# Modulation as plain float32 products in four column tiles

## The chip, the cores and the metric

The kernel runs on one core of one Trainium2 chip. The metric is the device time of one execution in microseconds; the median of three runs of the kernel before is 2310.57 us (2305.61 to 2311.26). TensorE (PE) multiplies, VectorE (DVE), ScalarE (ACT) and GpSimd (POOL) work elementwise, and SyncE (SP) issues most of the DMAs, in order.

## The reference

One inference step of a two-layer trunk on 128 context tokens and 512 latent tokens of width 1024, all in float32. In each layer the input is normalised and modulated, `h = rms_norm(x, g) * (1 + scale) + shift`; `h` goes through one wide projection into four mixers (two softmax attentions with several heads, a differential attention, a state-space scan), gates, and merges; the result is projected and added back, `x = x + gate * out`.

What matters here is where `shift`, `scale` and `gate` come from:

```
sh, sc, ga = split(silu(c) @ w_mod[l] + b_mod[l], 3)     # once for the context c_ctx, once for the latent c
```

`w_mod[l]` is 1024 x 3072 in float32, so each layer multiplies two vectors by a 12.6 MB matrix.

## The kernel before, in words

Activations are held feature-major, 128 features by 640 tokens. Products are made to float32 precision out of float32r operands: each operand is split into a high part (`fhi`, rounded by ACT, line 130) and a low part (`flo`, the difference, line 131, on the engine that is passed in), and three products hi·hi, hi·lo, lo·hi are added (lines 148 to 152). `w_chunk` (line 133) does that for a 256 KB block of weights: a DMA on SP into a raw tile (`fraw`), ACT makes `fhi`, POOL or DVE makes `flo`. The tag `f` has 3 raw buffers and 4 of each part, and is used by gates, merges, branch outputs and several projections (`fm_halves`, line 699: 48 matmuls of 320 columns for two blocks, in two halves, 0.146 us apart).

`modulation(l, part)` (line 214) makes one third of the modulation of a layer. For each half `ch` of 512 output columns it takes 8 blocks of 128 x 512 weights. Each block is split, and the four columns of `s4` (high and low parts of the two conditioning vectors) are the stationary operand: one matmul of 512 columns against `hi` (line 229) and one against `lo` (line 230), into 4 rows of a PSUM bank. The rows are copied or added to `row` (lines 232, 234), four 4 x 128 transposes (line 239) turn them to columns, and three to five small DVE operations finish `mod` (lines 241 to 248).

It is called in two ways.

- With `pool`, ahead of layer 0: parts 0 and 1 (shift and scale), 32 blocks with tag `m` (8 raw buffers, 4 of each part), all eight blocks of a half in one accumulation. The low parts go to DVE for two blocks in three and to POOL for the third. This stage is ordered by the compiler's planner on every engine. `h` (lines 1317 to 1319) waits for both parts of its half, and the first projection (`tm_proj`, lines 174 to 176) for `h`.
- Without `pool`, beside the gates and merges (tag `f`): part 2 of layer 0 and parts 0 and 1 of layer 1 in layer 0, part 2 of layer 1 in layer 1: 64 blocks, two to an accumulation, so 32 bursts of four matmuls. `mix(project(3, 0), chain(*mod), 8)` puts a burst after every eight steps of the merge and branch-output products; these in turn are dealt out between the pieces of the attentions by `fill`. From the end of the first stage on, PE runs in the order in which the program is written; the other engines and the DMA queues are still ordered by the planner.

Of the kernel before, what the change touches and what calls it, by code (L numbers as in the profile page):

```python
# [12 lines left out]
F32 = mybir.dt.float32  # L13
F32R = mybir.dt.float32r
AF = mybir.ActivationFunctionType
ALU = mybir.AluOpType
AX = mybir.AxisListType

P = 128
DEPTH = 2  # L20
D = 1024
KD = 8
# [3 lines left out]
TC = (0, 128, 384, 512, 256)  # L26
EPS = 1e-6
MLA_SCALE = 96 ** -0.5
WB = {"w": (2, 2), "f": (3, 4), "m": (8, 4)}
PTB = 3  # L30
PB = 2
TB = 3
# [23 lines left out]
def hybrid_kernel(ctx: ExitStack, tc: tile.TileContext, A, O, dbg=None):  # L56
    nc = tc.nc
    V, S, G, T = nc.vector, nc.scalar, nc.gpsimd, nc.tensor

    cp = ctx.enter_context(tc.tile_pool(name="cp", bufs=1))  # L60
    wp = ctx.enter_context(tc.tile_pool(name="wp", bufs=2))
# [5 lines left out]
    def nm(s):  # L67
        uid[0] += 1
        return f"{s}_{uid[0]}"

    def taker(pool):
        def take(tag, shape, bufs=1, dt=F32):
            return pool.tile(shape, dt, tag=tag, name=nm(tag), bufs=bufs)
        return take

    ct = taker(cp)

    def f(ap):
        return ap.bitcast(F32)

    def load(dst, src):
        nc.sync.dma_start(dst, src)
        return dst
# [6 lines left out]
    ident = ct("ident", [P, P])  # L90
# [18 lines left out]
    def psum_mm():  # L109
        return ps.tile([P, 512], F32, tag="mm", name=nm("mm"), bufs=2)  # L110
# [17 lines left out]
    def split_to(hi, lo, src, eng=V):  # L128

        S.activation(hi, src, AF.Copy)  # L130
        eng.tensor_tensor(lo, src, f(hi), ALU.subtract)  # L131

    def w_chunk(src, shape, eng=V, t="w", pool=wp):

        raw = load(pool.tile(shape, F32, tag=t + "raw", name=nm(t + "raw"), bufs=WB[t][0]), src)
        hi, lo = (pool.tile(shape, F32R, tag=t + n, name=nm(t + n), bufs=WB[t][1]) for n in ("hi", "lo"))
        split_to(hi, lo, raw, eng)
        return hi, lo
# [66 lines left out]
    sT = ct("sT", [P, KD, 2])  # L205
    S.activation(sT, cc, AF.Tanh, scale=0.5)
    V.scalar_tensor_tensor(sT, sT, 1.0, cc, op0=ALU.add, op1=ALU.mult)
    V.tensor_scalar(sT, sT, 0.5, None, op0=ALU.mult)
    s4 = ct("s4", [P, KD, 2, 2], 1, F32R)
    split_to(s4[:, :, :, 0], s4[:, :, :, 1], sT)  # L210

    mods = {}

    def modulation(l, part, group=2, pool=None):


        mod = mods[l, part] = ct(f"mod{part}", [P, KD, 2], 2)
        gcol = load(ct("gcol", [P, KD], 2), A["ng"][l]) if part == 1 else None
        bm = load(ct("bm", [P, KD], 2), A["bmod"][l, part])
        pt = ct("mpt", [P, KD, 4], 2)  # L220
        for ch in range(2):
            row = ct("mrow", [4, 512])
            for k0 in range(0, KD, group):
                acc = psum_mm()
                for k in range(k0, k0 + group):
                    src = A["wmod"][l, 2 * part + ch, k]
                    whi, wlo = w_chunk(src, [P, 512], V if k % 3 else G, "m", pool) if pool else w_chunk(src, [P, 512], G, "f")
                    lhs = s4[:, k].rearrange("p a b -> p (a b)")
                    T.matmul(acc[0:4, :], lhsT=lhs, rhs=whi, start=k == k0, stop=False)
                    T.matmul(acc[0:4, :], lhsT=lhs, rhs=wlo, start=False, stop=k == k0 + group - 1)  # L230
                if k0 == 0:
                    S.activation(row, acc[0:4, :], AF.Copy)
                else:
                    V.tensor_tensor(row, row, acc[0:4, :], ALU.add)
                if not pool:
                    yield
            tr = psum_mm()
            for q in range(4):
                T.transpose(tr[:, 4 * q:4 * q + 4], row[:, q * P:(q + 1) * P], ident[0:4, 0:4])
            c = slice(4 * ch, 4 * ch + 4)  # L240
            V.tensor_copy(pt[:, c], tr[:, 0:16].rearrange("p (m s) -> p m s", s=4))
            pv, m = pt[:, c].rearrange("p m (s t) -> p m s t", t=2), mod[:, c]
            V.tensor_tensor(m, pv[:, :, :, 0], pv[:, :, :, 1], ALU.add)
            V.tensor_tensor(m, m, bm[:, c].unsqueeze(2).to_broadcast([P, 4, 2]), ALU.add)
            if part == 1:
                V.scalar_tensor_tensor(m, m, 1.0, gcol[:, c].unsqueeze(2).to_broadcast([P, 4, 2]), op0=ALU.add, op1=ALU.mult)
            if part == 2:
                V.tensor_scalar(m, m, 0.25, None, op0=ALU.mult)
            if pool:
                yield  # L250
# [1038 lines left out]
    acc = xat("acc", [P, NT])  # L1289
# [12 lines left out]
    for l in range(DEPTH):  # L1302
# [3 lines left out]
        if l == 0:  # L1306
            mstack, mp = open_pool("m0")
            first = [modulation(0, i, KD, mp) for i in range(2)]
# [4 lines left out]
        for k in range(KD):  # L1313
            sh, sc = mods[l, 0], mods[l, 1]
            t = xat("ht", [P, NT], 2)
# [57 lines left out]
        for i in range(8):  # L1373
            nc.sync.dma_start(ucm[64:80, :, i], usb[16 * i:16 * i + 16])
            src = outs[i // 2][64 * (i % 2):64 * (i % 2) + 64].rearrange("p (g n) -> p g n", n=16)
# [20 lines left out]
        for ft in range(4):  # L1396
# [3 lines left out]
            pv = py[:, :, 0:320].rearrange("p h (i c) -> p h i c", c=80)  # L1400
# [29 lines left out]
        kstack, kp = open_pool(f"k{l}")  # L1430
        at = lambda tag, *a, takers=(taker(bp), taker(kp)): takers[tag in ("k", "q", "v")](tag, *a)
        mod = [modulation(l, 2)] + ([] if last else [modulation(l + 1, i) for i in range(2)])

        def project(n, i):
# [5 lines left out]
        b = []  # L1440
# [22 lines left out]
        for d_ in range(KD):  # L1463
            bo = fm_tile(A["wbo"][l, 1, d_], *b, 4, G)
            t = load(xat("ht", [P, NT], 2), ttd[l][1][d_])
            pv = load(xat("sq", [P, NT], 2), mgd[l][2][d_])
# [5 lines left out]
        acc = xat("acc", [P, NT])  # L1472
# [22 lines left out]
def cols(x):  # L1495

    t, f_ = x.shape
    return x.reshape(t // 8, 8, f_)[:, ::-1].reshape(t // 8, 2, 4, f_).transpose(1, 2, 0, 3).reshape(2, t // 2, f_)
# [17 lines left out]
def host_inputs(x):  # L1516
    x = {k: np.asarray(v) for k, v in x.items()}
    c = np.ascontiguousarray
    o = {}
# [20 lines left out]
    w = x["w_in"]  # L1540
    a = np.cumsum([0, 256, 128, 32, 512, 512, 512, 512, 128, 128, 512, 2048, 4096])
# [44 lines left out]
    b = np.stack([x["ssm_b_re"], x["ssm_b_im"]], 1)  # L1586
# [18 lines left out]
    def tmj(t):  # L1605
        return c(cols(t).reshape(4, P, -1).transpose(1, 0, 2))

    o["tk"] = c(np.stack([np.concatenate([tmj(cF), tmj(cM)], -1), np.concatenate([tmj(sF), tmj(sM)], -1)], 1))
    o["blk"] = c(np.repeat(np.eye(4, dtype=np.float32), 32, 0))
    return o  # L1610

# [39 lines left out]
```

## Time and profile before

| | |
|---|---|
| median of three runs | 2310.57 us |
| profiled execution | 2309.3 us, span 2307.5 us |
| granted TensorE clock, mean | 0.961 of full speed |
| PE busy | 2109.0 us (91%) |
| DVE busy | 1375.3 us (60%) |
| ACT busy | 1031.0 us (45%) |
| POOL busy | 905.1 us (39%) |
| DMA | 400.60 MB, mean 174 GB/s |

The busy share is a mean over stages. In the view of stretches a row gives its bounds in us, its length, the busy us of each engine with the count of instructions, the granted clock (1.00 is 2.4 GHz), the share of the DMA engines that was busy, and the rate. Matmuls overlap in the pipeline, so the cost of one in a stream is read from the difference of two starts, not from its duration.

### The profile page before, as it was taken

The numbers are of one execution on the slowest core, as the hardware profiler recorded it, in microseconds if no ns is written. First come the engines' busy times: TensorE is split into PE (matmuls) and PEld (weight loads), VectorE is DVE, ScalarE is ACT, GpSimd is POOL, SyncE is SP. The second block draws the span as 40 slices with busy tenths as digits, with TensorE's granted clock in tenths as the row PEclk, the third lists the DMA queues.
The fourth block names the chain that finished last, engine by engine and source line by source line (L and its number), as shares of the span: only waits on it lengthen the run. The fifth ranks groups of instructions, "written<-read, shape, count | busy, mean of one in ns | idle before, by whom it ended". The sixth has DMA issues, their size and how long they took to land. (4 is left out here: it accounts for less than half of the span.)

```text
span 2307.5 us, 38266 instructions
## 1 busy us (share of the span) xinstructions
PE 2109.0 (91%) x14197; PEld 2010.3 (87%) x14197; DVE 1375.3 (60%) x2515; ACT 1031.0 (45%) x2069; POOL 905.1 (39%) x637
## 2 busy tenths in 40 slices
PE   5876889969999999998799999997999999999997
PEld 2876789969998889998788999897899899999997
DVE  7998672755455455665777685349345455565542
ACT  5332343314556665553233444341346656554332
POOL 4477431312335552345553364232132523234522
PEclk9988999989999999999899999998999999999998
DMA  6455576533745666666473386763384455566643
GB/s 219 118 189 200 183 240 189 175 90 120 214 140 152 179 193 181 182 196 198 155 252 129 117 249 217 248 180 93 102 249 131 148 149 156 174 188 184 201 148 116
DMA packets 238635, 400.60 MB, mean 174 GB/s; under 512 B 36400, under 2 KB 110128, under 8 KB 238448
## 3 DMA queue, kind: packets, MB, share of 16 engines
q1 hardware_dynamic: 224208, 372.13, 53.5%
q10 hardware_dynamic: 14240, 26.02, 3.1%
q8 instruction: 111, 1.82, 0.4%
q14 instruction: 76, 0.62, 0.1%
HBM read 279.67 MB, written 117.87 MB: 172 GB/s over the span
## 5 line engine op out<-in xcount | busy, mean ns | idle before, releaser
L131 POOL TENSOR_TENSOR flo<-fraw,fhi 128x512 fp32r<-128x512 f32 x368 | 528.4, 1443 | 897.4 <-ACT fhi L130 850.4
L148 PE MATMUL mm<-hhi,fhi 128*128 128x320 f32 x2048 | 667.2, 326 | 25.2 <-DVE gt L764 7.5
L152 PE MATMUL mm<-hhi,flo 128*128 128x320 f32 x2048 | 640.8, 313 | 7.0 <-POOL flo L131 7.0
L150 PE MATMUL mm<-hlo,fhi 128*128 128x320 f32 x2048 | 639.8, 312 | 0.0
L148 PEld LDWEIGHTS mm<-hhi,fhi 128*128 128x128 f32 x2048 | 393.7, 192 | 38.3 <-ACT rx L942 8.0
L152 PEld LDWEIGHTS mm<-hhi,flo 128*128 128x128 f32 x2048 | 391.2, 191 | 8.2 <-POOL flo L131 8.0
L150 PEld LDWEIGHTS mm<-hlo,fhi 128*128 128x128 f32 x2048 | 392.9, 192 | 0.8
L130 ACT ACTIVATE fhi<-fraw 128x512 fp32r<-128x512 f32 x368 | 228.2, 628 | 166.3 <-PE mm L150 102.7
L131 DVE TENSOR_TENSOR ptl<-sm,pth 128x512 fp32r<-128x512 f32 (+1 forms) x240 | 142.4, 621 | 166.0 <-ACT pth L130 165.7
L786 DVE TENSOR_REDUCE mx<-s 128x1 f32<-128x640 f32 (+1 forms) x240 | 167.4, 714 | 106.2 <-PE s L819 51.2
L131 POOL TENSOR_TENSOR wlo<-wraw,whi 128x512 fp32r<-128x512 f32 (+1 forms) x80 | 117.7, 1474 | 219.9 <-ACT whi L130 205.6
L130 ACT ACTIVATE pth<-sm 128x512 fp32r<-128x512 f32 (+1 forms) x240 | 122.2, 543 | 126.7 <-PE sm L846 97.6
L819 PE MATMUL s<-k,q 128*128 128x384 f32 (+5 forms) x1008 | 159.1, 305 | 2.6 <-ACT p L788 1.8
L819 PEld LDWEIGHTS s<-k,q 128*128 128x128 f32 (+1 forms) x1008 | 155.0, 189 | 3.5 <-ACT p L788 2.1
L130 ACT ACTIVATE whi<-wraw 128x512 fp32r<-128x512 f32 (+1 forms) x96 | 59.1, 617 | 168.1 <-PE s L150 88.2
L148 PE MATMUL mm<-bh,fhi 128*128 128x320 f32 x384 | 126.2, 329 | 5.5 <-DVE gt L764 3.6
L717 ACT ACTIVATE gt<-mm 128x320 f32<-128x320 f32 x192 | 83.0, 432 | 90.4 <-PE mm L152 88.7
L846 PE MATMUL sm<-ident,p 128*128 128x128 f32 x800 | 116.0, 274 | 7.9 <-DVE ptl L131 2.9
L869 PE MATMUL sm<-pth,v 128*128 128x256 f32 (+1 forms) x528 | 120.4, 282 | 0.3 <-ACT pth L130 0.3
L152 PE MATMUL mm<-bh,flo 128*128 128x320 f32 x384 | 119.8, 312 | 0.0
L150 PE MATMUL mm<-bl,fhi 128*128 128x320 f32 x384 | 119.8, 312 | 0.1
L869 PE MATMUL sm<-ptl,v 128*128 128x256 f32 (+1 forms) x440 | 112.6, 281 | 0.5 <-DVE ptl L131 0.5
(425 smaller groups left out, 4170.7 us busy)
## 6 DMA issues: line engine op xcount, KB each, us to landing
fraw<-in_wmerge SPq DMA_DIRECT2D x128, 256.0 KB, 3.0
fraw<-in_wgate SPq DMA_DIRECT2D x64, 256.0 KB, 2.9
fraw<-in_wmod SPq DMA_DIRECT2D x64, 256.0 KB, 2.8
mgd<-gt SPq DMA_DIRECT2D x48, 320.0 KB, 2.8
fraw<-in_wbo SPq DMA_DIRECT2D x48, 256.0 KB, 3.0
k<-dkd SPq DMA_DIRECT2D x64, 192.0 KB, 4.0
gtd<-gt SPq DMA_DIRECT2D x32, 320.0 KB, 3.3
pv<-mgd SPq DMA_DIRECT2D x32, 320.0 KB, 3.8
```

The source lines that it names most:

```text
L130: S.activation(hi, src, AF.Copy)
L131: eng.tensor_tensor(lo, src, f(hi), ALU.subtract)
L148: T.matmul(outs[i], lhsT=whi, rhs=mhis[i], start=first, stop=False)
L150: T.matmul(outs[i], lhsT=whi, rhs=mlos[i], start=False, stop=False)
L152: T.matmul(outs[i], lhsT=wlo, rhs=mhis[i], start=False, stop=last)
L717: S.activation(t[:, r[0]], r[1], AF.Tanh, scale=0.5)
L786: V.tensor_reduce(mx[:, 0:1], s, axis=AX.X, op=ALU.max, negate=True)
L819: T.matmul(o, lhsT=tok(q, t), rhs=k[:, a:b], start=i == 0, stop=i == n - 1)
L846: T.transpose(pt[:, a:a + P], p[:, jj, P * kt:P * kt + P], ident)
L869: T.matmul(o, lhsT=v, rhs=p_, start=n == 0, stop=n == len(todo) - 1)
```

## The change

All 96 blocks of the modulation are multiplied as plain float32, with no split. The stationary operand is `s32`, 32 columns for each feature block, two of them the conditioning vectors and 30 zero. A matmul takes 256 of a block's 512 columns. The two blocks of a pair and their two halves make four matmuls, and each writes its own 32 partitions of one PSUM bank, at 0, 32, 64 and 96. The four parts of the sum, 128 rows of 256 columns, are copied or added to `row` as before, and a matmul against a constant 0/1 matrix `pick` adds the rows of the two blocks and turns them to columns: two matmuls of 4 columns in place of four transposes. One DVE operation adds the bias straight from PSUM.

Ahead of layer 0 the raw tiles have 16 buffers in place of 8, and the 4 + 4 buffers of the parts are gone. Beside gates and merges the two raw blocks of a pair are loaded by DMA straight into one `fhi` and one `flo` buffer of tag `f`; no `fraw` buffer, no ACT copy and no POOL subtraction is used.

```diff
-WB = {"w": (2, 2), "f": (3, 4), "m": (8, 4)}
+WB = {"w": (2, 2), "f": (3, 4), "m": 16}
...
-    s4 = ct("s4", [P, KD, 2, 2], 1, F32R)
-    split_to(s4[:, :, :, 0], s4[:, :, :, 1], sT)
+    s32 = ct("s32", [P, KD, 32])
+    V.memset(s32, 0.0)
+    V.tensor_copy(s32[:, :, 0:2], sT)
+    pick = load(ct("pick", [P, 4]), A["pick"])
...
-            row = ct("mrow", [4, 512])
+            row = ct("mrow", [P, 256])
             for k0 in range(0, KD, group):
                 acc = psum_mm()
-                for k in range(k0, k0 + group):
-                    src = A["wmod"][l, 2 * part + ch, k]
-                    whi, wlo = w_chunk(src, [P, 512], V if k % 3 else G, "m", pool) if pool else w_chunk(src, [P, 512], G, "f")
-                    lhs = s4[:, k].rearrange("p a b -> p (a b)")
-                    T.matmul(acc[0:4, :], lhsT=lhs, rhs=whi, start=k == k0, stop=False)
-                    T.matmul(acc[0:4, :], lhsT=lhs, rhs=wlo, start=False, stop=k == k0 + group - 1)
+                for k in range(k0, k0 + group, 2):
+                    raws = [mp_.tile([P, 512], dt, tag=t, name=nm(t), bufs=n) for mp_, t, n, dt in
+                            ([(pool, "mraw", WB["m"], F32)] * 2 if pool else [(wp, "f" + x, WB["f"][1], F32R) for x in ("hi", "lo")])]
+                    raws = [load(r if pool else f(r), A["wmod"][l, 2 * part + ch, k + i]) for i, r in enumerate(raws)]
+                    for i in range(2):
+                        for h in range(2):
+                            j = 2 * i + h
+                            T.matmul(acc[32 * j:32 * j + 32, 0:256], lhsT=s32[:, k + i], rhs=raws[i][:, 256 * h:256 * h + 256],
+                                     start=k == k0, stop=k == k0 + group - 2)
...
-            for q in range(4):
-                T.transpose(tr[:, 4 * q:4 * q + 4], row[:, q * P:(q + 1) * P], ident[0:4, 0:4])
+            for q in range(2):
+                T.matmul(tr[:, 4 * q:4 * q + 4], lhsT=row[:, q * P:(q + 1) * P], rhs=pick, start=True, stop=True)
...
-            V.tensor_copy(pt[:, c], tr[:, 0:16].rearrange("p (m s) -> p m s", s=4))
-            pv, m = pt[:, c].rearrange("p m (s t) -> p m s t", t=2), mod[:, c]
-            V.tensor_tensor(m, pv[:, :, :, 0], pv[:, :, :, 1], ALU.add)
-            V.tensor_tensor(m, m, bm[:, c].unsqueeze(2).to_broadcast([P, 4, 2]), ALU.add)
+            m = mod[:, c]
+            V.tensor_tensor(m.rearrange("p (h q) s -> p q h s", h=2), tr[:, 0:8].rearrange("p (q h s) -> p q h s", q=2, h=2),
+                            bm[:, c].rearrange("p (h q) -> p q h", h=2).unsqueeze(3).to_broadcast([P, 2, 2, 2]), ALU.add)
```

## Rows read from the trace of the kernel before

**Rows 1.** The page: busy us, share and instructions of each engine.
```profile
PE 2109.0 (91%) x14197; PEld 2010.3 (87%) x14197; DVE 1375.3 (60%) x2515; ACT 1031.0 (45%) x2069; POOL 905.1 (39%) x637
```

**Rows 2.** Stretches of 20 us near the start: PE, PEld, DVE, ACT, POOL busy, clock, DMA.
```profile
20.00:40.00 20.00, 14.71 (x50) 4.08 (x48) 15.43 (x22) 13.35 (x26) 9.62 (x7) 0.91 0.73 226
40.00:60.00 20.00, 15.04 (x62) 9.06 (x63) 19.81 (x31) 12.20 (x24) 10.91 (x8) 0.83 0.44 130
...
160.00:180.00 20.00, 13.35 (x79) 12.81 (x79) 20.00 (x27) 7.06 (x13) 16.04 (x7) 0.83 0.68 232
```

**Rows 3.** Stretches of 40 us before and among the modulation's bursts in layer 0.
```profile
620.00:660.00 40.00, 39.43 (x288) 39.06 (x287) 21.05 (x49) 24.21 (x54) 10.99 (x8) 1.00 0.39 121
...
700.00:740.00 40.00, 37.45 (x256) 33.05 (x256) 21.76 (x45) 24.55 (x50) 22.99 (x18) 1.00 0.53 156
```

**Rows 4.** Groups by shape, first 62 us: busy us, mean ns, idle before.
```profile
L130 ACT ACTIVATE mhi<-mraw 128x512 fp32r<-128x512 f32 x32 | 18.5, 619 | 2.1 <-DVE mlo L131 1.1 <-PE mm L229 0.8 <-issue 0.2
L131 POOL TENSOR_TENSOR mlo<-mraw,mhi 128x512 fp32r<-128x512 f32 x12 | 17.6, 1464 | 28.8 <-ACT mhi L130 26.3 <-PE mm L229 2.4
L131 DVE TENSOR_TENSOR mlo<-mraw,mhi 128x512 fp32r<-128x512 f32 x20 | 17.1, 882 | 4.1 <-ACT mhi L130 4.1
...
L243 DVE TENSOR_TENSOR mod<-mpt 128x8 f32<-128x8 f32 x4 | 2.8, 688 | 0.1
```

**Rows 5.** A stretch of 4 us in which the DMA engines are full.
```profile
12.00:16.00 4.00, 2.00 (x10) 2.00 (x10) 1.74 (x3) 3.06 (x5) 1.62 (x1) 1.00 1.04 386
```

**Rows 6.** Instructions in order of time, first stage: start us, us, engine, line.
```profile
21.02 0.63 PE L229 MATMUL mm<-mhi,s 128*4 128x512 f32 x1
...
21.45 0.63 PE L230 MATMUL mm<-mlo,s 128*4 128x512 f32 x1
...
37.05 0.17 DVE L246 SCALAR_TENSOR_TENSOR mod<-mod,gcol 128x8 f32<-128x8 f32 x1
...
52.99 0.35 PE L174 MATMUL s<-whi,hhi 128*128 128x416 f32 x1
...
55.93 0.16 DVE L246 SCALAR_TENSOR_TENSOR mod<-mod,gcol 128x8 f32<-128x8 f32 x1
```

**Rows 7.** Single lines, early: ns min/median/max, first and last start us.
```profile
L1319 DVE SCALAR_TENSOR_TENSOR hlo<-ht,mod,hhi x16: 340/739/1802, 39.4 to 71.7; 128x512 fp32r<-128x512 f32 x8, 128x128 fp32r<-128x128 f32 x8
...
L176 PE MATMUL mm<-whi,hlo x8: 345/348/353, 56.2 to 79.8; 128*128 128x416 f32 x8
```

**Rows 8.** In order of time: a burst beside the merges, and another's end.
```profile
683.85 0.31 PE L152 MATMUL mm<-hhi,flo 128*128 128x320 f32 x1
684.00 0.40 PE L229 MATMUL mm<-fhi,s 128*4 128x512 f32 x1
...
684.70 0.39 PE L230 MATMUL mm<-flo,s 128*4 128x512 f32 x1
...
684.93 0.30 PE L148 MATMUL mm<-hhi,fhi 128*128 128x320 f32 x1
...
690.01 0.39 PE L230 MATMUL mm<-flo,s 128*4 128x512 f32 x1
...
690.37 0.42 PE L148 MATMUL mm<-bh,fhi 128*128 128x320 f32 x1
```

**Rows 9.** In order of time: plain float32 products with 16 stationary columns.
```profile
1298.72 0.31 PE L152 MATMUL mm<-hhi,flo 128*128 128x320 f32 x1
1298.96 0.39 PE L488 MATMUL sm<-WY,BB 128*16 128x128 f32 x2
...
1300.50 0.38 PE L489 MATMUL sm<-WY,BB 128*16 128x128 f32 x2
1300.81 0.41 PE L148 MATMUL mm<-hhi,fhi 128*128 128x320 f32 x1
```

**Rows 10.** The page: POOL's costliest group, and the modulation's DMAs beside the merges.
```profile
L131 POOL TENSOR_TENSOR flo<-fraw,fhi 128x512 fp32r<-128x512 f32 x368 | 528.4, 1443 | 897.4 <-ACT fhi L130 850.4
...
fraw<-in_wmod SPq DMA_DIRECT2D x64, 256.0 KB, 2.8
```

More of the change, by code (lines that the diff above doesn't have):

```diff
@@ L219, in modulation @@
         bm = load(ct("bm", [P, KD], 2), A["bmod"][l, part])
-        pt = ct("mpt", [P, KD, 4], 2)
         for ch in range(2):
-            row = ct("mrow", [4, 512])
+            row = ct("mrow", [P, 256])
             for k0 in range(0, KD, group):
                 acc = psum_mm()
-                for k in range(k0, k0 + group):
-                    src = A["wmod"][l, 2 * part + ch, k]
-                    whi, wlo = w_chunk(src, [P, 512], V if k % 3 else G, "m", pool) if pool else w_chunk(src, [P, 512], G, "f")
-                    lhs = s4[:, k].rearrange("p a b -> p (a b)")
-                    T.matmul(acc[0:4, :], lhsT=lhs, rhs=whi, start=k == k0, stop=False)
-                    T.matmul(acc[0:4, :], lhsT=lhs, rhs=wlo, start=False, stop=k == k0 + group - 1)
+                for k in range(k0, k0 + group, 2):
[7 more added lines that the diff above has]
+                                     start=k == k0, stop=k == k0 + group - 2)
                 if k0 == 0:
-                    S.activation(row, acc[0:4, :], AF.Copy)
+                    S.activation(row, acc[:, 0:256], AF.Copy)
                 else:
-                    V.tensor_tensor(row, row, acc[0:4, :], ALU.add)
+                    V.tensor_tensor(row, row, acc[:, 0:256], ALU.add)
                 if not pool:
@@ L1608, in host_inputs @@
     o["tk"] = c(np.stack([np.concatenate([tmj(cF), tmj(cM)], -1), np.concatenate([tmj(sF), tmj(sM)], -1)], 1))
+    pick = np.zeros((2, 2, 32, 2, 2), np.float32)
+    for h in range(2):
+        for s in range(2):
+            pick[:, h, s, h, s] = 1.0
+    o["pick"] = pick.reshape(P, 4)
     o["blk"] = c(np.repeat(np.eye(4, dtype=np.float32), 32, 0))
```

## The prediction, made before the changed kernel ran

> **What bounds the kernel now.** I read the page's line of busy times first, then the busy times by stretch, then single instructions where the modulation stands. The line says PE 91%, DVE 60%, ACT 45%, POOL 39% [rows 1], but that is a mean over two quite different regimes. At the start PE is not the bound: from 20 to 60 us it is busy 14.7 and 15.0 of 20 us, partly at a lower granted clock (0.91 and 0.83), while DVE goes from 15.4 to 19.8 of 20; at 160 to 180 us DVE is at 20.00 of 20 and PE at 13.4 [rows 2]. So the first 200 us are paced by DVE, and by the moment at which `h` exists. Beside the merges it is the other way round: just ahead of the bursts PE is busy 39.4 of 40 us at full clock, and among them 37.5 of 40 [rows 3]. There a microsecond of PE is a microsecond of the kernel, and work taken from ACT and POOL is worth only what it takes out of PE's 2.5 us of idle. The change therefore has two sums of its own, one for each place.
>
> **Ahead of layer 0: what goes.** 32 high parts on ACT (18.5 us), 12 low parts on POOL (17.6), 20 on DVE (17.1) and one of the small DVE operations after the transposes, 4 times (2.8) [rows 4]. None of it is replaced. DVE, which paces this stretch, is thus relieved of 17.1 + 2.8 = 19.9 us.
>
> What is late next is the DMA. The stage must load `x`, 8 x 320 KB = 2.6 MB, and 32 blocks of 256 KB = 8.4 MB. Before, raw buffers came free only after a split; now 16 of them come free when PE has read them. With the engines full the trace moves 386 GB/s [rows 5]. From about 3 us, `x` and the first half of the blocks (6.8 MB) take 17.6 us, to 21 us; all of it (11.0 MB) takes 28.5 us, to 32 us. I add 1 us for the last pair and 3 us for the row, the turn to columns and the small operations (before, some 3 to 4 us from the last product). Shift and scale of the first half are then there at 25 us and those of the second at 36 us, where before the last operation on them started at 37.05 and 55.93 [rows 6]: 12 and 20 us earlier.
>
> Does PE keep up? A pair of blocks arrives every 2 x 262 KB / 386 GB/s = 1.36 us [rows 5]. A plain float32 product of 128 columns costs 0.22 us at full clock: eight starts from 1298.96 to 1300.50, (1300.50 - 1298.96) / 7 [rows 9]. One of 256 columns I take at twice that, 0.44 us, so a pair costs 1.74 us if its four products follow each other, and 0.87 if two run at a time (below). At the lower level, at which the old products also ran here (0.43 us from start to start for 512 columns at 21 us, against 0.23 beside the merges [rows 6, 8]), it would be twice as much. In my forecast PE is just ahead of the DMA at 2.4 GHz and somewhat behind at 1.2.
>
> How much of the 12 to 20 us is kept? The first projection started on PE at 52.99 [rows 6], its last matmuls at 79.8, and the last `hlo` at 71.7 [rows 7]. `h` itself is DVE work: per block of features two pairs of operations of 0.74 and 0.34 us, 8 x 2 x 1.08 = 17 us [rows 7]. From 25 us, with the second half from 36, that ends at about 46, some 26 us earlier; PE can start 12 to 16 us earlier. Between these and DVE's 19.9 us I take 16 us, with bounds of 4 (DVE, POOL and DMA work of the next stage doesn't move forward with `h`) and 25. After it PE's order is fixed and PE mostly busy, so I let the gain stand to the end. **-16 us.**
>
> **Beside the merges: PE.** An old burst is four products of 512 columns: starts at 684.00, ..., 684.70, and the next work at 684.93, so 0.23 each and 0.93 in all; another ends with 0.36 in place of 0.23 [rows 8]. I take 1.0 us. A new burst is four products of 256 columns. The trace shows a plain float32 product as two instructions (x2 a product [rows 9]), each with its own weight load, so 8 x 0.22 us of array time. No matmul before writes to PSUM partitions other than 0 up, so no row shows how products in different column tiles overlap, and the price must be bounded. From below, all four at once: 0.44 us. From above, one after the other: 8 x 0.22 = 1.76 us. I take a middle way: instructions start in order, the second half of a product must wait for the first half in the same tile, and only the first half of the next product, in another tile, runs beside it. That is 5 x 0.22 = 1.1 us. Going in and out costs more than before: the narrow float32 products of the trace stand 0.24 us behind their predecessor (0.15 is the usual distance) and the next work 0.31 behind the last (0.22), so 0.09 each [rows 9]. New burst 1.1 + 0.18 = 1.28 us, 0.28 more than before; 32 bursts: **+9 us.**
>
> Against the change speaks the Trainium skill, "TensorEngine Tiling (Array Packing)", section "Key Properties": changing the tiling mode, as opposed to the tile, drains the array. If a drain is what a matmul lasts beyond its pitch, 0.38 - 0.22 = 0.16 us [rows 9], two of them a burst would cost an estimated 10 us in place of the 5.8 us that I have by the rows' 0.09; the old four-column bursts show from 0 to 0.13 [rows 8].
>
> **Beside the merges: the rest.** 64 splits leave ACT, and 64 low parts of 1443 ns leave POOL [rows 10], 92 us of POOL. PE idles 2.5 of 40 us among the bursts and 0.6 ahead of them [rows 3]; the layer-0 bursts cover some 172 us, so at most 4 x 1.9 = 8 us could come back. I take 2, since part of that idle is the wait for the row, which stays. Rows of 128 x 256 in place of 4 x 512, two float32 products with `pick` (four instructions) in place of four transposes: nothing, hidden beside merge products that don't depend on them; without that cover 16 + 48 of them cost perhaps 0.1 us each.
>
> The new wait is that a pair's DMA now needs a free `fhi` and `flo` buffer, which PE frees, where it needed `fraw`, which POOL freed. It sits on SP's queue, behind it all later loads (weights, gates, keys). The pair takes one slot of four instead of two, and the slot it needs belonged to a block at least half a merge unit back, 24 x 0.146 = 3.5 us of PE work; a DMA lands 2.8 us after issue [rows 10]. I cost it at nothing; were it bare, it is 2.8 us for some bursts, 10 us at most. **-2 us.**
>
> **Sum.** 2309.3 (the profiled execution) - 16 + 9 - 2 = 2300.3; it lies 1.3 us under the median shown, less than a measurement tells, so I say 2300.
>
> **Rivals.**
> *A. All four tiles run at once.* A burst is 0.44 + 0.18 = 0.62, 0.38 less than before, -12 us over 32; the first stage is as above. 2309 - 16 - 12 - 2 = 2279. For it: nothing forbids that a second half waits in its own tile while the others start. Against it: the order of the program, half by half. The Trainium skill, "TensorE: Matmul & The Clock Gate", section "Part 3: Packing small matmuls — row/col tiling", has it so: a pack lasts one matmul and some 4 ns for each further tile. Its matmuls are of one instruction each, and no run here shows it yet.
> *B. They run one by one.* The array takes one moving stream of float32 at a time. A burst is 1.76 + 0.18 = 1.94, +30 us over 32 bursts, in the stretch where PE is the bound. In the first stage PE becomes the bound, 16 x 1.74 = 28 us from about 11: halves at 28 and 42, and of the gain 11 us remain. 2309 - 11 + 30 - 2 = 2326, slower. It decides from a burst of 1.4 us on. For it: products in one tile follow each other exactly [rows 9]; against it only that other tiles are other columns.
> *C. The early gain is swallowed.* `h` comes early, but DVE's 20 of 20 us at 160 to 180 [rows 2] is prep work of the state-space branch in an order that the planner sets anew, and PE waits for that as late as before. 2309 + 9 - 2 = 2316, or 2312 with the bound of 4 us.
>
> **Chances and range.** Forecast 0.36, A 0.24, B 0.20, C 0.20. A measurement of this kernel tells 0.3%, 7 us, from no change: faster is below 2304, slower above 2317.5. The forecast's own spread is 2290 to 2309, and three quarters of it are faster. Faster: 0.27 + 0.23 of A + 0.04 of the rest = 0.54. Same: 0.09 + 0.12 of C + 0.03 of B = 0.24. Slower: 0.16 of B + 0.06 of C = 0.22. The range takes in A and half of B: 2275 to 2326.
>
> **What would show it.** First stage: no splits of the modulation left on ACT, DVE and POOL, DMA at over 350 GB/s to about 32 us, the two last operations on the scale at about 25 and 36 us, the first projection at 37 to 41. If that start is early and the stretch at 160 to 200 us is not, C holds. Beside the merges: from the matmul before a burst to the one behind it 1.3 us in the forecast, 0.6 in A, 1.9 in B. PE's busy share of 40 us among the bursts should rise over 37.5. Loads that land late ahead of a burst would show the new wait. The prediction is wrong if the bursts are as forecast and the start not at least 10 us earlier, or the other way round.

## The result, and the profile after

The changed kernel takes **2283.59 us** (median of 4 runs, 2282.58 to 2285.21) against 2309.01 us for the kernel before on the same chip (4 runs, 2305.61 to 2311.26): ratio 0.9892, 95% interval 0.9875 to 0.9909, 25 us faster. The forecast was 2300 us, in a range of 2275 to 2326. The profiled execution has a span of 2282.2 us against 2307.5; lines beyond the modulation have numbers higher by six (L717 is now L723, L1319 is now L1325).

Busy us of each engine on the page; it answers to [rows 1]. PE has 192 instructions more and 21 us less, POOL 107 us less, ACT 57, DVE 28:

```profile
PE 2087.9 (91%) x14389; PEld 2006.0 (88%) x14389; DVE 1347.0 (59%) x2472; ACT 974.3 (43%) x1972; POOL 797.7 (35%) x561
```

The stretches, in the columns of [rows 2, 3 and 5]: PE, PEld, DVE, ACT, POOL busy, granted clock, DMA share, GB/s.

```profile
20.00:40.00 20.00, 13.32 (x123) 6.48 (x114) 8.24 (x20) 5.52 (x13) 0.00 (x0) 0.84 0.81 287
40.00:60.00 20.00, 16.11 (x73) 14.68 (x74) 18.79 (x32) 9.01 (x19) 11.40 (x10) 0.91 0.43 129
160.00:180.00 20.00, 14.22 (x89) 13.42 (x88) 19.76 (x26) 5.97 (x12) 16.06 (x8) 0.91 0.71 224
...
700.00:740.00 40.00, 37.73 (x292) 33.95 (x291) 17.11 (x37) 17.60 (x37) 8.24 (x6) 1.00 0.49 148
...
28.00:32.00 4.00, 1.85 (x32) 0.85 (x32) 3.83 (x10) 1.65 (x3) 0.00 (x0) 1.00 1.05 387
32.00:36.00 4.00, 1.04 (x8) 1.02 (x12) 3.47 (x8) 2.41 (x5) 0.00 (x0) 0.68 0.76 215
36.00:40.00 4.00, 3.55 (x32) 1.30 (x32) 0.78 (x3) 0.70 (x3) 0.00 (x0) 0.50 0.16 59
```

DMA runs full to 32 us (387 GB/s in 28:32, while PE and DVE work). Among the bursts PE is busy 37.73 of 40 us, where it was 37.45: two operations a burst fewer on ACT, and two fewer on POOL, have hardly raised it. In 32:36 PE is busy only 1.04 of 4 us and the granted clock falls to 0.68; in 36:40, where the last products of the first stage run, it is 0.50, the level of 1.2 GHz.

Instructions in order of time, first the first stage, then one burst beside the merges with its neighbours; they answer to [rows 6 and 8]:

```profile
23.17 3.61 PE L236 MATMUL mm<-mraw,s 128*32 128x256 f32 x32
27.91 1.94 PE L236 MATMUL mm<-mraw,s 128*32 128x256 f32 x32
28.23 0.17 DVE L252 SCALAR_TENSOR_TENSOR mod<-mod,gcol 128x8 f32<-128x8 f32 x1
34.55 0.36 ACT L239 ACTIVATE mrow<-mm 128x256 f32<-128x256 f32 x1
34.96 1.02 PE L246 MATMUL mm<-pick,mrow 128*128 128x4 f32 x4 [5.11 <-ACT mrow L239]
35.91 3.64 PE L236 MATMUL mm<-mraw,s 128*32 128x256 f32 x32
40.65 0.43 PE L174 MATMUL s<-whi,hhi 128*128 128x416 f32 x1
41.03 0.66 DVE L252 SCALAR_TENSOR_TENSOR mod<-mod,gcol 128x8 f32<-128x8 f32 x1
...
666.48 0.31 PE L152 MATMUL mm<-hhi,flo 128*128 128x320 f32 x1
666.72 0.41 PE L236 MATMUL mm<-fhi,s 128*32 128x256 f32 x2
666.73 0.41 PE L236 MATMUL mm<-flo,s 128*32 128x256 f32 x2
666.96 0.39 PE L236 MATMUL mm<-fhi,s 128*32 128x256 f32 x2
666.97 0.39 PE L236 MATMUL mm<-flo,s 128*32 128x256 f32 x2
667.45 0.41 PE L148 MATMUL mm<-hhi,fhi 128*128 128x320 f32 x1
```

Each row of a burst holds two instructions (x2), so four start within 0.02 us, and four more 0.24 us later. The scale of the first half is worked on at 28.23 us (37.05 before), that of the second at 41.03 (55.93), and the first projection starts at 40.65 (52.99).

Where the 25 us came from, by the start of the same work in both traces, after less before: first projection -12.3 us; first work on the scan's states -13.6; first scores of layer 0's attention -17.1 (567.5 against 584.6); last scores there -22.8 (1041.3 against 1064.1); first matmul of the last column sums, near the end, -26.2 (2263.5 against 2289.7). About two thirds are the first stage; 5.7 us (22.8 less 17.1) are gained while layer 0's attention, with 24 of the 32 bursts, runs. In the rest the difference wanders between -15.8 and -26.2, and the last 9 us of it come at 2100 to 2200 us, of which more below.

### The profile page after: what moved, and what is told of

Its sections match the earlier page's. It is cut to its first block, busy times and chain, and to the rows that moved or that the text cites. A ratio compares the mean times of both kernels' runs of the same rounds, so it can differ in the third digit from the quotient of the medians.

```text
span 2282.2 us, 38357 instructions
## 1 busy us (share of the span) xinstructions
PE 2087.9 (91%) x14389; PEld 2006.0 (88%) x14389; DVE 1347.0 (59%) x2472; ACT 974.3 (43%) x1972; POOL 797.7 (35%) x561
## 5 line engine op out<-in xcount | busy, mean ns | idle before, releaser
L131 POOL TENSOR_TENSOR flo<-fraw,fhi 128x512 fp32r<-128x512 f32 x304 | 436.6, 1440 | 958.1 <-ACT fhi L130 878.7
L130 ACT ACTIVATE fhi<-fraw 128x512 fp32r<-128x512 f32 x304 | 190.1, 629 | 145.7 <-PE mm L150 103.7
L852 PE MATMUL sm<-ident,p 128*128 128x128 f32 x800 | 115.7, 274 | 5.6 <-DVE ptl L131 3.3
L723 ACT ACTIVATE gt<-mm 128x320 f32<-128x320 f32 x192 | 82.9, 432 | 86.8 <-PE mm L152 81.9
```

Of the source, the lines that this page charges most:

```text
L723: S.activation(t[:, r[0]], r[1], AF.Tanh, scale=0.5)
L852: T.transpose(pt[:, a:a + P], p[:, jj, P * kt:P * kt + P], ident)
```

## The experiments

Times are medians; each ratio is to runs of the kernel before on the same chip. "Burst total" is the time from the start of the row of PE's timeline ahead of a burst to the start of the first matmul behind it, summed over all 32 bursts: 47.2 us before, 41.9 in the changed kernel. The row ahead of some bursts holds several matmuls (for six, the turn of a finished row to columns), and their time is in the total; counted from the last single matmul it is 45.2 and 39.6.

**Which part does it?** Two kernels with one half of the change each; the other place keeps the old function.

```diff
...
+    def modulation(l, part, group=2, pool=None):
+        return (mod_new if bool(pool) == True else mod_old)(l, part, group, pool)    # first_only; False in merge_only
```

> Only the stage ahead of layer 0 is changed; the bursts beside the merges are the old ones. Theory 1 (the early gain is kept to the end, the bursts add a few us): the state-space scan's first product starts 13 to 14 us earlier than before (at 381 in place of 394.5) and the kernel ends 14 us earlier, about 2295 us. Theory 2 (the bursts bring nothing, since what they save becomes a wait): about 2286, as in the full change. Theory 3 (rival C, the early gain is swallowed): within 4 us of before.

> Only the bursts beside the merges are changed; the stage ahead of layer 0 is the old one. Theory 1 (half of what a shorter burst saves turns into a wait of the next product for its PSUM bank): 5 to 6 us less than before, about 2303 us; bursts of 0.57 us where nothing is waited for, and a wait of 0.3 to 0.8 us on the tanh of the gate (line 723 of the changed kernel) behind about half of them. Theory 2 (nothing is left): 2309. Rival A at its full price: 2295.

Only the first stage new: 2287.91 us, ratio 0.9901 [0.9882, 0.9919]. Only the bursts new: 2302.52, ratio 0.9962 [0.9944, 0.9979], burst total 41.7 us. So the new bursts are faster than the old ones and not slower: the sign of my +9 is refuted. The first stage alone has its projection 12.1 us earlier, the scan's states 13.0, the scores of attention 14.9 to 15.4 earlier, from the first to the last; at the end it is 23.0 by the medians. That time is the second theory's, but not for its reason, since the new bursts gain by themselves. The medians of the parts, -23.0 and -8.3 us, come to 6 us more than the -25.4 of both; with intervals of 18.7 to 27.3 and 4.9 to 12.9 us that doesn't show that the parts fail to add up.

**Do tiles run side by side, or is each product merely cheap?** The same float32 products without column tiles: one product of 512 columns for each block, all in partitions 0 to 31. The row (32 x 512) and its turn to columns (four products) are fitted to it.

```diff
...
-                        for h in range(2):
-                            j = 2 * i + h
-                            T.matmul(acc[32 * j:32 * j + 32, 0:256], lhsT=s32[:, k + i], rhs=raws[i][:, 256 * h:256 * h + 256], ...)
+                        T.matmul(acc[0:32, :], lhsT=s32[:, k + i], rhs=raws[i], start=k + i == k0, stop=k + i == k0 + group - 1)
...
```

> Plain float32 and everything else as in the change, but no column tiles: each block is one product of 512 columns into partitions 0 to 31. Theory 1 (the column tiles run at once, and that is what makes plain float32 cheap): a burst takes 8 x 0.22 + 0.1 = 1.9 us in place of 0.57, with no wait for PSUM behind it, 0.8 us more per burst on average, 26 us over 32; the first stage takes 28 us of PE at full clock, halves of the scale at 30 and 45 us; about 2316 us, slower than before. Rival (PE waits anyway for the bank of the merge product, so the length of a burst hardly matters): within 6 us of the full change, 2284 to 2290.

2326.23 us, ratio 1.0066 [1.0049, 1.0083], burst total 73.5. A burst in order of time:

```profile
691.79 0.31 PE L152 MATMUL mm<-bh,flo 128*128 128x320 f32 x1
692.03 1.04 PE L234 MATMUL mm<-fhi,s 128*32 128x512 f32 x2
692.91 1.02 PE L234 MATMUL mm<-flo,s 128*32 128x512 f32 x2
693.86 0.42 PE L148 MATMUL mm<-hhi,fhi 128*128 128x320 f32 x1
```

One after the other the same sums take 1.83 us (692.03 to 693.86), against the old 0.93 [rows 8] and 0.57 for four tiles at once where nothing is waited for (680.41 to 680.98, shown further below). The column tiles are what makes this change faster; plain float32 alone is 0.7% slower than before. The first theory holds in kind; its 2316 us was 10 too low, with 31.6 us more of bursts than in the changed kernel where 26 were expected, and first scores 10.5 us later. In the first stage the projection starts only 1.3 us earlier here, and yet the scan's states come 7.0 us earlier: what this kernel shares with the changed one is the work taken from DVE. I read it so that about half of the changed kernel's 13.6 us there is relief of DVE, and the other half the earlier `h`; no run takes the two apart.

**Does the order of the program hold a tile back?** Each block in a tile of its own, its two halves one behind the other, so that products stand in the order 0, 0, 1, 1. The row (64 x 512) and its turn to columns (four products) are fitted to it.

```diff
...
-                            j = 2 * i + h
-                            T.matmul(acc[32 * j:32 * j + 32, 0:256], ...)
+                            T.matmul(acc[32 * i:32 * i + 32, 256 * h:256 * h + 256], ...)
...
```

> The change with two column tiles in place of four: each block has its own 32 partitions, and its two products of 256 columns go into them one behind the other, so the order of the program is tile 0, 0, 1, 1. Theory 1 (each tile takes its own products as it becomes free, whatever stands between them): four halves of 0.22 us in each tile, side by side, a burst of 0.88 + 0.13 = 1.0 us; the kernel about 2288. Rival (the forecast's middle way: an instruction that waits for its tile holds up those behind it, so only the ends overlap): 7 x 0.22 + 0.13 = 1.67 us a burst, the kernel at about 2305.

2300.12 us, ratio 0.9962 [0.9948, 0.9977]. A burst in order of time:

```profile
676.59 0.31 PE L152 MATMUL mm<-hhi,flo 128*128 128x320 f32 x1
676.83 0.40 PE L238 MATMUL mm<-fhi,s 128*32 128x256 f32 x1
676.84 0.40 PE L238 MATMUL mm<-flo,s 128*32 128x256 f32 x1
677.07 0.38 PE L238 MATMUL mm<-fhi,s 128*32 128x256 f32 x1
677.08 0.38 PE L238 MATMUL mm<-flo,s 128*32 128x256 f32 x1
...
677.50 0.38 PE L238 MATMUL mm<-fhi,s 128*32 128x256 f32 x1
677.51 0.38 PE L238 MATMUL mm<-flo,s 128*32 128x256 f32 x1
677.82 0.42 PE L148 MATMUL mm<-hhi,fhi 128*128 128x320 f32 x1
```

The block of `flo` stands behind all four instructions of `fhi` in the program, and its first one starts 0.01 us after the first of `fhi`. Here program order does not hold back another tile; that it does was the assumption of my middle way. (The trace gives starts and not places in PE's stream; that the stream keeps the order of the source is taken from the way the kernel is built.) The body is 0.99 us, four steps of some 0.22 us in place of two, as the first theory has it. Its time of 2288 us was 12 too low: the burst total is 8.3 us over the changed kernel's, and the first stage, which the theory left out, is slower too (projection at 46.64 us, first scores 10.3 us later).

**What took part of the saving back?** Behind more than half of the new bursts (20 of 32) the next merge product starts over 0.08 us late. Waits of PE in 640:850 of the changed kernel (line, what it waited for: us in all, times, longest):

```profile
PE mm L148 <- ACT gt L723: 3.4, 7, 0.7
PE mm L236 <- DVE mod L249: 1.5, 2, 0.8
PE mm L148 <- DVE gt L770: 1.4, 3, 0.7
```

The tag `mm` has two PSUM banks; a burst takes one, and the next merge unit needs the one that ACT or DVE is still reading out (`gt`). The edit puts the burst's bank into the tag `sm`:

```diff
-                acc = psum_mm()
+                acc = psum_mm() if pool else psum1()
```

> The change, with one edit: the bursts beside the merges accumulate in the PSUM tag of the attention (sm) and not in that of the merge products (mm), which has two banks. Theory 1 (the wait behind a burst is for the second mm bank): no burst is followed by a wait on the tanh of the gate, all of them last 0.57 to 0.73 us, 8 us less than the full change, about 2275. Rival (the banks are short everywhere): the wait moves to the transposes and values of the attention, 2280 to 2290.

2274.13 us (2268.07 to 2276.76), ratio 0.9832 [0.9811, 0.9853], beside the changed kernel's 0.9892 [0.9875, 0.9909]: **faster than both kernels**. Burst total 32.8 us, 9.1 less than in the changed kernel, and the time is 9.5 us less by the medians (14 by the ratios, since the two ran beside different runs of the kernel before). The wait on ACT's `gt` is gone and that on DVE's is down to 0.2, in the same view and stretch:

```profile
PE mm L148 <- DVE gt L770: 0.2, 1, 0.2
```

Is the wait new? The same edit on the kernel before (its accumulator of four rows in `sm`):

> The kernel before with one edit: the accumulator of the old four-product bursts beside the merges lies in the PSUM tag sm in place of mm (the edit that took the changed kernel from 2283.6 to 2274.1 us). The bursts of before last 47.2 us in all (from the matmul ahead of each to the next product), 12.7 more than 32 undisturbed ones of 1.08. Theory 1, the wait for the second bank of mm belongs to the mixing of bursts with merges and was there before the change: old_sm gains as much as acc_sm did, 7 to 10 us, 2299 to 2302, and its bursts sum to some 37 us. Theory 2, the wait is what the shorter bursts ran into (half of their saving given back): old_sm gains at most 4 us, 2305 or more, and its bursts stay above 43 us.

2301.34 us, ratio 0.9976 [0.9963, 0.9989], burst total 41.7: it gains 5.5 us in the bursts and some 6 in time. That lies between the two theories. The wait was there before, nearly as large. Waits of PE in 655:870 of the kernel before:

```profile
PE mm L148 <- ACT fhi L130: 1.1, 2, 0.8
PE mm L148 <- ACT gt L717: 1.0, 3, 0.4
PE mm L229 <- DVE gt L764: 0.9, 1, 0.9
```

Many delays are too short to appear there as idle time, so I count the starts: the time by which the product behind a burst comes later than behind an undisturbed one is 8.3 us over the 32 old bursts (16 of them late by more than 0.08 us) and 10.9 us over the new ones (20). With the bank in `sm` it is 2.2 us (2 bursts) and 1.4 us (3). The shorter burst only runs into the wait somewhat more often.

With the bank in `sm` the burst total falls by 41.7 - 32.8 = 8.9 us from the old product to the new, in the shared bank by 47.2 - 41.9 = 5.3. Of these, 3.0 and 1.9 us are given back one product later, where the total no longer looks: behind a new burst the second merge product stands 0.25 us behind the first, behind an undisturbed old one 0.15. Counted to that second product, the new burst is worth 5.9 us in `sm` and 3.4 in `mm`.

**Where do the raw blocks lie?** The pair into two of the three `fraw` buffers, in place of one `fhi` and one `flo`:

```diff
-                            ([(pool, "mraw", WB["m"], F32)] * 2 if pool else [(wp, "f" + x, WB["f"][1], F32R) for x in ("hi", "lo")])]
+                            ([(pool, "mraw", WB["m"], F32)] * 2 if pool else [(wp, "fraw", WB["f"][0], F32)] * 2)]
...
```

> The change, but the raw blocks beside the merges are loaded into the raw buffers (fraw, 3 of them) and not into the tiles of the high and low parts. Theory 1 (the place matters: a pair holds two of three raw buffers until PE has multiplied it, so the loads of the merges' blocks come late): PE waits for the splits of the merges, 5 to 10 us more than the full change, 2289 to 2294. Rival (loads have slack either way): within 2 us of the full change, 2282 to 2286.

2315.51 us, ratio 1.0032 [1.0019, 1.0045]: 32 us slower than the changed kernel, where the first theory had 5 to 10, and slower than before. Layer 0's attention, first to last scores, takes 496.9 us against 473.8. Its waits in 640:870, first PE's, then those of SP's queue of DMAs:

```profile
PE mm L152 <- POOL flo L131: 7.8, 12, 0.8
PE mm L148 <- ACT fhi L130: 4.0, 6, 1.1
...
SPq L82 <- POOL flo L131: 49.2, 26, 4.8
SPq L82 <- PE mm L236: 46.9, 19, 4.6
```

Loads of merge blocks stand on SP's queue behind a modulation pair that waits for PE to leave a `fraw` buffer; then PE waits for the splits of those blocks, which come late. In the changed kernel neither wait on the splits is among the larger ones of PE, and SP's queue has no wait on L236; its wait on `flo` is the larger there (88.0 us), so that row alone tells nothing. The two rows of PE make up 11.8 of the 23.1 us by which the attention is longer.

**What holds the first stage?** Ahead of layer 0 the third row's products are done at 29.85 us (they start at 27.91 and take 1.94), but ACT copies the row at 34.55, behind its work for `h` (`hhi`), and PE stands idle for 5.11 us at L246 for it. The edit issues those ACT operations behind the copies of the third and fourth rows; the second kernel has it with the burst's bank in `sm`.

```diff
...
+                with tc.issue_after(rows_in[2 if k < 2 else 3].ins) if l == 0 else ExitStack():
                     S.activation(v_(hhi[:, k]), v_(t), AF.Identity, bias=sh[:, k, s_:s_ + 1])
```

> The change, with one edit ahead of layer 0: ScalarE's operations on h are ordered behind its copies of the third and fourth row of the modulation. In the changed kernel the third row is copied at 34.55 us although its products ended near 30, because ScalarE's queue had h's operations first, and PE idled 5.1 us for it. Theory 1 (that wait sets when the first projection starts): it starts at 35 to 36 us in place of 40.65, and 3 to 5 us of it reach the end, about 2280. Rival (VectorE's work behind it is the bound, and a PE that starts earlier only waits later): the scan's first product within 1 us of 380.9, and the end within 2 us of 2283.6.

> Both edits together: bursts that accumulate in the attention's PSUM tag, and the rows ahead of h. If the two gains are of different places they add: 2274 - 4 = 2270. If the early edit brings nothing: 2274.

2284.75 us, ratio 0.9895 [0.9881, 0.9908], and 2279.75, ratio 0.9873 [0.9856, 0.989]. The copy moves to 30.25, the scale of the second half to 37.22, and the scan's states come 2.7 us earlier than in the changed kernel; the projection starts at 38.62, 2.0 us earlier, where 35 to 36 was expected, and DVE's last `hlo` at 52.35 against 52.53, hardly earlier, as the rival has it. At the end this isn't told apart from the changed kernel: a gain of 3 us at 400 us is below what such a comparison resolves. The second confirms the bank's move in direction (5 us in this comparison, 9.5 in the other). Whether the two edits add stays open: by the medians both together are slower than the bank's move alone, by the profiled executions 1.9 us faster (spans of 2272.2 and 2274.1), and the runs of both together lie between 2272.3 and 2282.1.

With 8 raw buffers ahead of layer 0 in place of 16:

```diff
-WB = {"w": (2, 2), "f": (3, 4), "m": 16}
+WB = {"w": (2, 2), "f": (3, 4), "m": 8}
```

> The changed kernel with 8 raw buffers ahead of layer 0 in place of 16. Theory 1, the DMA is what paces the first stage and needs only a few free buffers, since PE frees a pair within 2 us of its landing: as the changed kernel, 2282 to 2287, the last operations on the scale within 1 us of 28.2 and 41.0. Theory 2, the run-ahead of 16 buffers counts, because the products stop while PE is at its lower clock or waits for a row: the scale of the second half 2 to 4 us later, the end 2 to 4 us later, 2286 to 2288.

2289.31 us (2282.97 to 2292.48), ratio 0.992 [0.9907, 0.9934]. The scales are worked on at 30.05 and 42.72 us, 1.8 and 1.7 later, and the projection starts 1.7 later. In 12:32 DMA moves 294 GB/s where the changed kernel moves 386. The trace agrees with the second theory for the first stage, though its delay is below the forecast 2 to 4 us; the interval overlaps the changed kernel's, so what the eight further buffers bring at the end stays open.

**What is the gain late in the kernel?** With only the first stage new, the difference grows from 15.4 us at the end of layer 0's attention in the trace to 23.0 by the medians (22.0 between the profiled executions), though nothing there is changed. The kernel before, profiled once more:

> The kernel before, profiled once more, unchanged, for its clock by stretch after 2080 us, where the first profile shows 0.67, 0.82, 0.91 and 0.75 in four stretches of 10 us and the kernel with only the new first stage shows 1.00. Theory 1, the drops belong to how the end of this kernel's order falls (PE waits there long enough each time): they come again at the same places. Theory 2, they come by chance of one execution: other places or none, and a span up to 5 us away from 2307.5.

2304.38 us, span 2302.6. Stretches of 10 us of the two executions of the kernel before, first the earlier one (columns as above):

```profile
2108.60:2118.60 10.00, 7.47 (x35) 6.87 (x34) 3.69 (x13) 5.14 (x13) 6.17 (x5) 0.67 0.86 266
2118.60:2128.60 10.00, 10.00 (x62) 10.00 (x61) 5.70 (x13) 3.82 (x10) 3.32 (x4) 0.82 0.46 148
```

```profile
2108.60:2118.60 10.00, 7.71 (x46) 7.43 (x45) 3.19 (x12) 6.40 (x14) 7.41 (x5) 0.83 0.69 221
2118.60:2128.60 10.00, 10.00 (x75) 9.99 (x74) 6.26 (x16) 4.19 (x11) 4.14 (x4) 1.00 0.76 232
```

The same kernel shows both: a gap at the same place (PE 7.47 and 7.71 of 10), after which one execution has two stretches at 0.67 and 0.82, and the other 0.83 and 1.00; a later drop to 0.75 in the first (2178.6 to 2188.6 us) does not come again (1.00). From the last scores of layer 0 to the first matmul of the last column sums, the two take 1225.6 and 1219.8 us; the changed kernel takes 1222.2, the one with only the first stage new 1218.1. So 6 us of a profile's second half can be scatter between executions of one and the same kernel, and against the second execution the changed kernel is 22.2 us earlier at the column sums and not 26.2. The medians hold more than that scatter: the kernel before ranged from 2302.6 to 2318.7 in all its runs, the changed one from 2282.6 to 2285.2 in its four, and the first stage alone gains 23 by its median where its trace shows 15.4 by the end of layer 0's attention. That the new start keeps later drops away is argued, not shown; some 2 to 7 us stay open.

## Why the prediction was right and where it was not

**The time** lay inside the range, the direction was right, but the likeliest value was 16 us too high: one term had the wrong sign. That the range held is no merit of that term; it had been drawn to take in rival A. By the sign that I had set (the start at least 10 us earlier, the bursts not as forecast) the mechanism was wrong in one of its two places.

**First stage, -16: held.** The trace shows -13.6 at the scan and -17.1 at the attention, and the kernel with this part alone -13.0 and -14.9. The path was as described: no splits left, DMA full to 32 us, PE's first projection at 40.65 (37 to 41 forecast). The scales were done 3 and 5 us later than forecast (28.2 and 41.0 against 25 and 36), and the last `hlo` starts at 52.5 where I had 46. I had named PE's lower clock, "somewhat behind at 1.2", but taken no time for it: at a granted clock of 0.50 the four packs (32 instructions) of the fourth row took 3.64 us, where those of the third row, at 1.00, took 1.94. Those of the second row went at the lower pace too, 3.61 us from 23.17, as the products of [rows 6] did at 21 us; the trace's first record of the clock is at 26.6 us, and the 1.00 that the view of stretches gives ahead of that is no reading. And the third row's copy stood behind ACT's own work for `h`, which I had not looked for. The bounds of 4 and 25 us were wide enough for both.

**Rival C: refuted.** DVE is still busy 19.76 of 20 us at 160 to 180 (20.00 in [rows 2]), but the work itself came forward with `h`: the last transposes of that preparation stand at 180.95 us, 10.7 earlier, and PE's work on the scan's states starts 13.6 earlier.

**Bursts, +9: the failed step.** "Only the first half of the next product, in another tile, runs beside it" was the step. The runs show in its place what rival A said: four tiles at once, second halves 0.24 us after the first ones, so that the products take 0.46 us where I had 1.1. The rule of the Trainium skill that I had named with A ("TensorE: Matmul & The Clock Gate", section "Part 3: Packing small matmuls — row/col tiling") agrees with the trace, though its matmuls are single instructions: starts in a pack lie within 0.02 us. I gave A a chance of 0.24 and the order of the program as reason against it; the two-tile kernel shows that this order doesn't bind.

The old burst was mis-sized too. I took 1.0 us from the two in [rows 8]; over all 32 it is 45.2/32 less a usual 0.15, 1.26 us, since the wait for the shared bank stands behind half of them. The new one in the same bank is 39.6/32 - 0.15 = 1.09 us, against 1.28 forecast. So the forecast's 0.28 us more a burst became 0.17 less (0.12 less when counted to the second product), and more than half of that turn is the old burst.

A's size was too large as well. It had 0.62 us for a burst; a burst that nothing disturbs, in the kernel with the bank in `sm`, runs like this:

```profile
680.18 0.31 PE L152 MATMUL mm<-bh,flo 128*128 128x320 f32 x1
680.41 0.41 PE L236 MATMUL sm<-fhi,s 128*32 128x256 f32 x2
680.43 0.41 PE L236 MATMUL sm<-flo,s 128*32 128x256 f32 x2
680.65 0.39 PE L236 MATMUL sm<-fhi,s 128*32 128x256 f32 x2
680.67 0.39 PE L236 MATMUL sm<-flo,s 128*32 128x256 f32 x2
680.98 0.41 PE L148 MATMUL mm<-hhi,fhi 128*128 128x320 f32 x1
681.23 0.30 PE L150 MATMUL mm<-hlo,fhi 128*128 128x320 f32 x1
```

In: 0.23 for a usual 0.15. Out: 0.33 from the last start where 0.22 is the pitch, and the product after that again 0.25 in place of 0.15. So 0.08 + 0.11 + 0.10 = 0.29 us beside the 0.46 of the products, 0.75 in all. The last 0.10 I had missed, though the kernel before has it at its narrow float32 products, behind the last row of [rows 9]:

```profile
1301.06 0.31 PE L150 MATMUL mm<-hlo,fhi 128*128 128x320 f32 x1
```

That is 0.25 us behind 1300.81. The old one took 0.93, from 683.85 to 684.93 less a usual 0.15 [rows 8]: 0.18 gained, 5.8 us over 32 bursts (5.9 measured above), where A had 0.38 and 12 us. The Trainium skill, "TensorEngine Tiling (Array Packing)", section "Key Properties", has two rules that bear on this. Tiles work independently of each other, which I had not weighed: the trace agrees, by the 0.01 us between starts in the two-tile kernel. And the array drains when the mode changes. Two drains of the 0.16 us that I had derived would be 0.32, near the row's 0.29; but no run here shows that the 0.29 is a drain. The narrow products of [rows 9], one behind the other in one place, have 0.09, 0.09 and 0.10, and behind the 128-column products of L852 the second merge product stands 0.23 us after the first (670.98 to 671.21), and so (0.23 in the median) in all 118 such places.

**The rest, -2.** 64 low parts went (POOL's group has 304 left, 436.6 us), and PE's idle among the bursts went only from 2.55 to 2.27 us of 40. The term can't be told apart from zero. What I had read as idle for lack of splits is in good part the shared PSUM bank, which no row of before that I quoted showed: in 655:870 the splits (`fhi`) hold 1.1 us and `gt` 1.9, and the bank's move took 5.5 us from the old bursts.

**The new wait, nothing: held, by the choice of tiles.** No wait of PE on a modulation DMA is among the larger ones beside the merges. What I did not price is what the choice of buffers is worth: the same pair in `fraw` buffers costs 32 us, three times my bound of 10.

**Rival B: refuted** for four tiles, and right in size for one: 1.83 us a burst (1.76 and the ways in and out, 1.94, forecast) and 2326.2 us, as B had it. That the time agrees to the microsecond is luck: the first stage kept 7 us where B had 11, and the bursts cost 26.3 where it had 30. (A pair in one tile is 4 x 0.44 = 1.76 us; the 1.74 is a slip that changes nothing.)

By the measured sizes the sum would have been 2309.3 - 13.6 to 17.1 (first stage) - 5.7 (bursts and the rest, during layer 0's attention) = 2287 to 2290; the profiled execution took 2284.3, and the 2 to 6 us between are within what the second half differs by from one execution to the next.

## What to carry to other kernels

Small plain-float32 products are worth packing into column tiles where a split would cost ACT and POOL time: four at once took a third of the time of the same work in one tile, and here the tiles needed no special order. After shortening a step on the bound engine, look at what its neighbours wait for: here a PSUM bank shared with them cost 8.3 us around the old bursts and 10.9 around the new, and moving it won 9.5 us by the medians (5 in another comparison). Price an old step from all its occurrences and not from two. Where transfers are given other buffers, ask which queue stands behind them before anything else: the same change with the wrong buffers was slower than before.

## What the runs showed that I had not expected

- Instructions of different column tiles start out of the order of the source: `flo` 0.01 us after `fhi`, though four instructions of `fhi`'s tile stand ahead of it; within a tile they follow each other every 0.21 to 0.24 us (676.83 to 677.50).
- The first ordinary product behind a burst of plain float32 products is followed 0.25 us later, not 0.15 (680.98 to 681.23), with tiles or without (1300.81 to 1301.06).
- One kernel's second half differs by 6 us between two executions, with other granted clocks around the same gap (0.67 and 0.82 against 0.83 and 1.00).
